# A decoder trunk on one core: gated values of two heads in products of 512 columns, memory tokens normed channel-major, some steps moved

## The chip, the core and the metric

The kernel runs on one core of a Trainium2 chip. The core has a matrix engine (TensorE, in the profile PE, with its weight loads PEld), VectorE (DVE), ScalarE (ACT), GpSimd (POOL) and SyncE (SP), which here only issues transfers. They run side by side, each through its own list of instructions in order, and wait for each other by semaphores. The metric is the device time of one execution in microseconds (us): 835.55 for the kernel before, the median of 3 runs (834.86 to 836.42).

## The reference, cut to what matters

```python
h = rmsnorm(x, g_pre)                       # x: 512 tokens x 1024 channels
gq, gk, gv, ga, gz, dq, dk, dv, iq, ik, iw, dz, xq, xz, gates = split_cols(h @ w_in)
y_gla = gla_mixer(gq, gk, gv, ga, gz, ...)  # 4 heads, chunks of 64; values gv: 256 columns a head
y_dsa = dsa_mixer(dq, dk, dv, iq, ik, iw, dz, rel_bias)  # top-k keys by an indexer
mem_n = rmsnorm(mem, g_mem)                 # 256 memory tokens x 1024 channels
mk, mv = split(mem_n @ w_mem_kv)
y_mem = cross_mixer(xq, xz, mk, mv)
merged = sum(sigmoid(gate) * (y @ w_out) for each branch)
out = x + rmsnorm(merged @ w_o, g_post)
```

All is float32. The norm is y * rsqrt(mean(y * y) + eps) * g over the 1024 channels of a token.

## The kernel before, in words

**Precision.** Each operand of a large product is split in two parts of a faster format: `high` (ScalarE, line 94) rounds, `low` (VectorE, lines 98 and 100) takes the rest. `mm3` (lines 107 to 109) then makes three products: high by high, first operand's high by second's low, low by high. With weights as the second operand its first product needs only whi, its second wlo.

**Weights and units.** Weights come in loads of 1 MB, two buffers (wraw), SyncE's queue. A load has two chunks; `split_next` makes whi (ScalarE) and puts the making of wlo (VectorE) on a list that `flush` works off after the next quarter of TensorE's work has been issued. whi and wlo have four buffers each, so a chunk's split waits until the chunk four before it was used. When a load's second chunk is split, the load after next is issued. Work on TensorE is a list of units of four quarters. A unit of `unit_t` has the channels of a chunk as weights and 512 tokens as moving columns: 24 products of 512 columns. A unit of `unit_n` (gv, dv, mv) has tokens as weights and 256 value columns as moving columns, two tiles of 128 tokens in one PSUM buffer: 48 products of 256 columns for gv, and both chunks of its load are used by each of the load's two units.

**Order.** `at(name, s, fn)` puts a step s quarters behind the start of a unit; s may go past 3, into later units. The loop at the end issues quarter, flush, splits of chunks to come (`need`), then, in the last quarter, the unit's `done`, then the steps of that place:

```python
if s == 1 and u < wo_first:
    need(u + 2)
if s == 3 and u + 2 < wo_first and chunks[u + 2][2]:
    need(u + 3)
```

The order of units at the start is dv, pc (indexer keys, gate inputs), gv0.0, gv0.1, gv1.0, gv1.1, iq0.0, iq0.1, iq1.0, iq1.1, gqk0, gz0, gqk1, gz1, gqk2, gv2, gz2, gqk3, gv3, gz3, dk, dq0. gv0 and gv1 work on x times the gain (gh, gl) and take the norm factor rstd of a token at the end; meanwhile `h_norm` makes the normed hh and hl that all later units use. `gv_done` splits the values to vh and vl. `dv_done` splits the other value products, which stand in four PSUM buffers since the start; `gate_operands` and `gate_log` prepare the forget gate (products pla), `gate_ln` and `gate_sum` finish it.

Of the gated attention's steps `gla_exps`, `gla_q` and `gla_k` (qd, kd, kte, kk) work on a head's gqk, `gla_att` makes its products pa, `gla_turn_k` the transposes tk, `gla_state` the state products kv, `gla_out` the outputs po with their squares, `gla_norm` scales them with GpSimd's rstd, `gla_y` turns and gates them. `score` and `topk_max`, `topk_drop` (16 rounds of three MAX8 and three MATCH_REPLACE8, from gz1.0 on, a step each three quarters) are the indexer's.

**Memory tokens.** `mem_load` (at gate12.0) loads the gain, repeated over the partitions, and two tiles of 128 tokens. At out14 and behind it each tile is squared (`norm_sq`), scaled (`norm_scale`) and turned by eight transposes (`norm_turn`, line 294, xps) into mh and ml, which the units mk and mv use from 559 us on.

**Start.** Channel-major x (xt, four tiles, the first in two halves from ScalarE's queue) and the weights of dv come first, then x token-major (four tiles), whose squares on ScalarE (line 1096) give rstd.

Of the kernel before, what the change touches and what calls it, by code (L numbers as in the profile page):

```python
# [10 lines left out]
F32 = mybir.dt.float32  # L11
# [6 lines left out]
D = 1024  # L18
# [24 lines left out]
for _h in range(4):  # L43
    _pair(f"gqk{_h}", OFF["gq"] + 128 * _h, OFF["gk"] + 128 * _h)
    for _n in ("gv", "gz", "dq", "dz", "xq", "xz"):
        _pair(f"{_n}{_h}", OFF[_n] + 256 * _h, OFF[_n] + 256 * _h + 128)
# [6 lines left out]
NORMAL = ("gv", "dv")  # L53
# [4 lines left out]
def trunk(ctx, tc, x, x_t, mem, w_in, w_c, w_kv, w_out, w_o, cols, g_mem, g_post, w_up, toe, out):  # L58
# [149 lines left out]

    hh = keep.tile([128, KT, T], F32R, name="hh", tag="hh")
# [57 lines left out]
    col = const.tile([128, 14], F32)  # L267
    ba, ggla, gpre = col[:, 0:4], col[:, 4:6], col[:, 6:14]
# [6 lines left out]

    def norm_sq(xt, xn):
        ss = s8("ss", 2)
        for i in range(2):
            act.activation(xn[i], xt[i], AF.Square, scale=1.0 / 32, accum_out=ss[:, i:i + 1])
        return ss  # L280

    def norm_scale(xt, xn, ss, g):
        v = s8("var", 1)
        dve.scalar_tensor_tensor(v, ss[:, 0:1], EPS, ss[:, 1:2], op0=OP.add, op1=OP.add)
        r = rstd_of(v, 1)
        for i in range(2):
            dve.scalar_tensor_tensor(xn[i], xt[i], r[:, 0:1], g[i], op0=OP.mult, op1=OP.mult)

    def norm_turn(xn, dst, tags=("tp", "tp")):
        pts = []  # L290
        for i in range(2):
            p = psum(tags[i], "xps")
            for j in range(4):
                pe.transpose(p[:, 128 * j:128 * j + 128], xn[i][:, 128 * j:128 * j + 128], ident)
            pts.append(p.rearrange("p (k t) -> p k t", k=4))
            high(dst(i)[0], pts[i])
        return lambda: [low(dst(i)[1], pts[i], dst(i)[0]) for i in range(2)]
# [77 lines left out]
    def gv_done(h, i, p):  # L375
        if i == 0:
            GV[h] = [w4(n, F32R).rearrange("p (t d) -> p t d", t=4) for n in ("vh", "vl")]
        vh, vl = GV[h]
        if h < 2:
            for j in range(2):  # L380
                tt = 2 * i + j
                split(vh[:, tt], vl[:, tt], p[:, 256 * j:256 * j + 256], R["rstd"][:, tt:tt + 1])
            return
# [807 lines left out]
```

## Time and profile before

| | before |
|---|---|
| median of 3 runs | 835.55 us |
| the profiled execution | 835.18 us |
| its span, first to last instruction | 833.5 us |
| granted TensorE clock, mean | 0.997 |
| TensorE busy | 818.7 us, 98% |
| weight loads (PEld) | 704.3 us, 85% |
| VectorE busy | 473.8 us, 57% |
| ScalarE busy | 337.1 us, 40% |
| GpSimd busy | 50.2 us, 6% |
| transfers | 86.30 MB, mean 104 GB/s |

Matmuls are pipelined: a product's duration in the profile is longer than the distance from its start to the next one's start, and it is that distance that counts for the stream. VectorE and ScalarE overlap a little too: the next operation starts some 0.1 us ahead of the end of the one before. The clock is TensorE's, as a share of 2.4 GHz; it has two levels, 1.2 and 2.4.

### The profile page before, as it was taken

The numbers are of one execution on the slowest core, as the hardware profiler recorded it, in microseconds if no ns is written. First come the engines' busy times: TensorE is split into PE (matmuls) and PEld (weight loads), VectorE is DVE, ScalarE is ACT, GpSimd is POOL, SyncE is SP. The second block draws the span as 40 slices with busy tenths as digits, with TensorE's granted clock in tenths as the row PEclk, the third lists the DMA queues.
The fourth block names the chain that finished last, engine by engine and source line by source line (L and its number), as shares of the span: only waits on it lengthen the run. The fifth ranks groups of instructions, "written<-read, shape, count | busy, mean of one in ns | idle before, by whom it ended". The sixth has DMA issues, their size and how long they took to land.

```text
span 833.5 us, 10783 instructions
## 1 busy us (share of the span) xinstructions
PE 818.7 (98%) x4320; PEld 704.3 (85%) x4320; DVE 473.8 (57%) x850; ACT 337.1 (40%) x608; POOL 50.2 (6%) x74
## 2 busy tenths in 40 slices
PE   7989999999999999999999999999999999999997
PEld 7989888989888888888888888889989898888885
DVE  4759677888686435446676543545655554343623
ACT  6577554453423223334444422334434343322320
POOL 1000010010000030032131000000000000000000
PEclk9999999999999999999999999999999999999999
DMA  9324121121222231222131125323324142226402
GB/s 332 117 102 138 51 91 62 52 101 53 100 101 101 101 105 73 101 104 99 51 108 71 51 101 176 101 101 101 112 92 147 56 152 70 86 98 223 156 1 102
DMA packets 16387, 86.30 MB, mean 104 GB/s; under 512 B 2064, under 2 KB 2576, under 8 KB 7760
## 3 DMA queue, kind: packets, MB, share of 16 engines
q1 hardware_dynamic: 15328, 84.02, 28.6%
q10 hardware_dynamic: 1008, 1.58, 0.5%
q8 instruction: 34, 0.56, 0.3%
q14 instruction: 17, 0.14, 0.0%
HBM read 82.42 MB, written 2.10 MB: 101 GB/s over the span
## 4 chain that ended last, share of the span: by engine, by line
PE 86%; DVE 5%; ACT 4%; DMA 2%; issue 2%; ACTq 0%; SPq 0%; DVEq 0%; POOLq 0%; POOL 0%
PE out L109 5%; PE out L107 5%; PE out L108 5%; PE pfin L109 2%; PE pfin L108 2%; PE pfin L107 2%; DVE wlo L98 1%; DMA x<-x 1%; PE tpp L721 1%; ACT whi L94 1%; DMA xt<-x_t 1%; PE pov L108 1%; PE pov L109 1%; PE lg L109 1%; PE lg L108 1%
## 5 line engine op out<-in xcount | busy, mean ns | idle before, releaser
L98 DVE TENSOR_TENSOR wlo<-wraw,whi 128x1024 fp32r<-128x1024 f32 (+1 forms) x135 | 163.4, 1211 | 84.4 <-ACT whi L94 83.5
L94 ACT ACTIVATE whi<-wraw 128x1024 fp32r<-128x1024 f32 (+1 forms) x135 | 139.4, 1039 | 22.2 <-PE out L108 19.6
L107 PE MATMUL out<-yh,whi 128*128 128x512 f32 x192 | 75.3, 392 | 0.0
L109 PE MATMUL out<-yh,wlo 128*128 128x512 f32 x192 | 74.8, 390 | 0.0
L108 PE MATMUL out<-yl,whi 128*128 128x512 f32 x192 | 74.8, 389 | 0.0
L707 ACT ACTIVATE bm<-bm,nm 128x128 f32<-128x128 f32 (+3 forms) x32 | 18.0, 564 | 73.6 <-DVE nm L705 71.8
L691 POOL TENSOR_TENSOR bm<-toe,madd 128x128 f32<-128x128 f32 (+3 forms) x32 | 31.0, 986 | 194.6 <-DMA toe<-toe 86.3
L109 PEld LDWEIGHTS out<-yh,wlo 128*128 128x128 f32 x192 | 36.0, 188 | 7.5
L107 PEld LDWEIGHTS out<-yh,whi 128*128 128x128 f32 x192 | 36.1, 188 | 7.3
L108 PEld LDWEIGHTS out<-yl,whi 128*128 128x128 f32 x192 | 36.1, 188 | 7.2
L94 ACT ACTIVATE yh<-th 128x512 fp32r<-128x512 f32 x16 | 10.1, 632 | 44.0 <-DVE th L657 24.9
L512 DVE SCALAR_TENSOR_TENSOR gth<-gth,out 128x512 f32<-128x512 f32 x16 | 11.0, 686 | 28.0 <-PE out L109 28.0
L273 POOL TENSOR_TENSOR rstd<-var,mhalf 128x1 f32<-128x1 f32 x6 | 3.3, 550 | 374.9 <-DVE var L952 289.7
L470 DVE MATCH_REPLACE8 madd<-m,madd 128x256 f32<-128x256 f32 (+2 forms) x48 | 25.6, 543 | 0.0
L466 DVE MAX8 m<-madd 128x8 f32<-128x256 f32 (+2 forms) x48 | 23.6, 546 | 0.0
L705 DVE CUSTOM_DVE_ANT_0 bm<-lg,bm 128x128 f32<-128x128 f32 (+3 forms) x32 | 15.5, 486 | 12.9 <-PE lg L109 12.7
L751 DVE TENSOR_TENSOR ydsa<-pov,th 128x128 f32<-128x128 f32 x32 | 7.8, 286 | 22.5 <-PE pov L109 22.1
L94 ACT ACTIVATE pth<-tpp 128x128 fp32r<-128x128 f32 (+3 forms) x32 | 13.7, 428 | 13.4 <-PE tpp L721 13.4
L456 DVE SCALAR_TENSOR_TENSOR madd<-relu,iw,madd 128x256 f32<-128x256 f32 (+2 forms) x21 | 12.9, 616 | 9.2 <-ACT relu L452 8.9
L949 ACT ACTIVATE sq<-pfin 128x512 f32<-128x512 f32 x8 | 4.8, 598 | 31.5 <-PE pfin L109 31.5
L98 DVE TENSOR_TENSOR yl<-th,yh 128x512 fp32r<-128x512 f32 x16 | 11.1, 693 | 11.2 <-ACT yh L94 11.2
L98 DVE TENSOR_TENSOR ptl<-tpp,pth 128x128 fp32r<-128x128 f32 (+3 forms) x32 | 15.5, 484 | 0.0
(1024 smaller groups left out, 2359.1 us busy)
## 6 DMA issues: line engine op xcount, KB each, us to landing
wraw<-w_in SPq DMA_DIRECT2D x43, 1024.0 KB, 4.8
wraw<-w_out SPq DMA_DIRECT2D x12, 1024.0 KB, 4.8
wraw<-w_kv SPq DMA_DIRECT2D x8, 1024.0 KB, 4.8
wraw<-w_o SPq DMA_DIRECT2D x4, 1024.0 KB, 4.8
x<-x SPq DMA_DIRECT2D x4, 512.0 KB, 8.2
toe<-toe SPq DMA_DIRECT2D x8, 256.0 KB, 5.2
xres<-x SPq DMA_DIRECT2D x4, 512.0 KB, 8.5
xt<-x_t SPq DMA_DIRECT2D x3, 512.0 KB, 7.6
```

The costliest lines, as they stand in the source:

```text
L94: act.activation(hi, src, AF.Copy, scale=scale)
L98: dve.tensor_tensor(lo, src, f(hi), op=OP.subtract)
L107: pe.matmul(o, lh, rh, start=first, stop=False)
L108: pe.matmul(o, lh, rl, start=False, stop=False)
L109: pe.matmul(o, ll, rh, start=False, stop=last)
L456: dve.scalar_tensor_tensor(sc, r[:, :n], iw[:, b, h:h + 1], sc, op0=OP.mult, op1=OP.add)
L466: dve.max(out=M8[b], in_=maskadd[b])
L470: dve.match_replace(out=maskadd[b], in_to_replace=M8[b], in_values=maskadd[b], imm_value=-FMAX)
L512: dve.scalar_tensor_tensor(th, th, 1.0, p, op0=OP.add, op1=OP.mult)
L691: pool.tensor_tensor(bm[:, :n], Q[hp]["toe"][i][:, 384 - 128 * qb:512], maskadd[qb], op=OP.add)
L705: dve.tensor_tensor_reduce(out=bm[:, :n], in0=lg[:, :n], in1=bm[:, :n], scale=-1.0, scalar=FMAX, op0=OP.add, op1=OP.min, accum_out=nm)
L707: act.activation(bm[:, :n], bm[:, :n], AF.Exp, scale=-1.0, bias=nm, accum_out=su)
```

## The change

- **Values of two heads.** gv leaves the pairs of `w_in`; its weights come as `w_gv`, four loads, in chunks of two channel tiles with 512 columns, that is two heads. `wide_units` makes four units for two heads (gvw0.0 to gvw0.3 for heads 0 and 1, gvw1.0 to gvw1.3 for heads 2 and 3), one for each 128 tokens; quarter q of every unit uses the group's chunk q. gvw0 stands where gv0 and gv1 stood; gvw1 stands where gv2 stood, and gv3's place is empty. `gv_done` makes one split of 512 columns per unit; the values lie in tiles of two token tiles by 512 columns, and `gv_of` picks a head's.
- **When chunks are split.** `ahead` replaces the two conditions quoted above: the first chunk of a group at the usual place, the second in the second quarter of the unit before the group, the third in that unit's last quarter, the fourth behind the group's first quarter; none in the next two units; in the group's last unit the next two chunks behind its first and second quarter.
- **Places.** `gate_operands` goes from the third quarter of gv0.1 to the first of gvw0.2, `dv_done` from gv1.0's four quarters to the four from gvw0.2's second on, `gate_log` to gvw0.3's quarters. The third head's `gla_att` and `gla_turn_k` go to gvw1.1; the fourth head gets the places of the second head, in gz3.0 and behind.
- **Memory tokens.** `mem_load` brings two tiles channel-major (`mem_t`) beside two token-major, in place of the repeated gain, which comes with `cols`. The token-major tiles are squared only, one operation of 1024 columns each; GpSimd's power of both; two products with the identity spread the factors over the partitions (`mem_row`, mrps); eight scalings of 256 columns and two splits of 1024 follow, a step a quarter. The transposes go.
- **Start.** The second half of the first xt tile goes to SyncE's queue, behind the first part of dv's weights.

```diff
-    for _n in ("gv", "gz", "dq", "dz", "xq", "xz"):
+    for _n in ("gz", "dq", "dz", "xq", "xz"):
...
-NORMAL = ("gv", "dv")
+NORMAL = ("dv",)
...
+    wide = set()
+
+    def wide_units(name, src, lhs, done):
+
+        first = len(units)
+        wide.add(first)
+        for i in range(2):
+            add_chunks(src[i], None)
+        for tt in range(4):
+            o = []
+
+            def quarter(q, tt=tt, o=o):
+                if q == 0:
+                    o.append(psum("mm", name))
+                wh, wl = chunks[first + q][3]
+                for k in (2 * q, 2 * q + 1):
+                    ah, al = lhs(k, tt)
+                    mm3(o[0], ah, al, wh[:, k % 2], wl[:, k % 2], k == 0, k == KT - 1)
+
+            unit(f"{name}.{tt}", quarter, lambda tt=tt, o=o: done(tt, o[0]))
...
-    col = const.tile([128, 14], F32)
-    ba, ggla, gpre = col[:, 0:4], col[:, 4:6], col[:, 6:14]
+    col = const.tile([128, 22], F32)
+    ba, ggla, gpre, gmem = col[:, 0:4], col[:, 4:6], col[:, 6:14], col[:, 14:22]
...
-    def norm_sq(xt, xn):
-        ss = s8("ss", 2)
-        for i in range(2):
-            act.activation(xn[i], xt[i], AF.Square, scale=1.0 / 32, accum_out=ss[:, i:i + 1])
-        return ss
...
-    def norm_scale(xt, xn, ss, g):
-        v = s8("var", 1)
-        dve.scalar_tensor_tensor(v, ss[:, 0:1], EPS, ss[:, 1:2], op0=OP.add, op1=OP.add)
-        r = rstd_of(v, 1)
-        for i in range(2):
-            dve.scalar_tensor_tensor(xn[i], xt[i], r[:, 0:1], g[i], op0=OP.mult, op1=OP.mult)
-
-    def norm_turn(xn, dst, tags=("tp", "tp")):
-        pts = []
-        for i in range(2):
-            p = psum(tags[i], "xps")
-            for j in range(4):
-                pe.transpose(p[:, 128 * j:128 * j + 128], xn[i][:, 128 * j:128 * j + 128], ident)
-            pts.append(p.rearrange("p (k t) -> p k t", k=4))
-            high(dst(i)[0], pts[i])
-        return lambda: [low(dst(i)[1], pts[i], dst(i)[0]) for i in range(2)]
 
 
...
-    def gv_done(h, i, p):
-        if i == 0:
-            GV[h] = [w4(n, F32R).rearrange("p (t d) -> p t d", t=4) for n in ("vh", "vl")]
-        vh, vl = GV[h]
-        if h < 2:
-            for j in range(2):
-                tt = 2 * i + j
-                split(vh[:, tt], vl[:, tt], p[:, 256 * j:256 * j + 256], R["rstd"][:, tt:tt + 1])
-            return
-        split(vh[:, 2 * i:2 * i + 2], vl[:, 2 * i:2 * i + 2], p.rearrange("p (t d) -> p t d", t=2))
-
-    for h in range(2):
-        win_n(f"gv{h}", lambda i, p, h=h: gv_done(h, i, p), g_lhs)
+    def gv_done(g, tt, p):
+        if tt == 0:
+            GV[g] = [[w4(n, F32R).rearrange("p (t d) -> p t d", t=2) for n in ("vh", "vl")]
+                     for _ in range(2)]
+        vh, vl = GV[g][tt // 2]
+        split(vh[:, tt % 2], vl[:, tt % 2], p, 1.0 if g else R["rstd"][:, tt:tt + 1])
+
+    def gv_of(h, p):
+        return [t[:, p % 2, 256 * (h % 2):256 * (h % 2) + 256] for t in GV[h // 2][p // 2]]
+
+    wide_units("gvw0", [w_gv[0], w_gv[1]], g_lhs, lambda tt, p: gv_done(0, tt, p))
...
-        at("gv1.0", tt, lambda tt=tt: dv_done(tt, R["dvps"][tt]))
+        at("gvw0.2", 1 + tt, lambda tt=tt: dv_done(tt, R["dvps"][tt]))
...
-    at("gv0.1", 2, gate_operands)
+    at("gvw0.2", 0, gate_operands)
     at("iq0.1", 2, turn_iw)
     for h in range(4):
-        at("gv1.1", h, gate_log, h)
+        at("gvw0.3", h, gate_log, h)
...
-        if h > 1:
-            win_n(f"gv{h}", lambda i, p, h=h: gv_done(h, i, p))
+        if h == 2:
+            wide_units("gvw1", [w_gv[2], w_gv[3]], h_lhs, lambda tt, p: gv_done(1, tt, p))
...
     def mem_load():
-        gm = w4("gm")
-        sp.dma_start(gm, bass.AP(tensor=g_mem.tensor, offset=g_mem.offset, ap=[[0, 128], [1, D]]))
-        R["gm"] = gm
-        R["mt"] = []
-        for tt in range(2):
-            mt = w4("mt")
-            sp.dma_start(mt, mem[128 * tt:128 * tt + 128])
-            R["mt"].append(mt)
-        for i in range(2):
+        R["mt"], R["mx"] = [w4("mt") for _ in range(2)], [w4("mx") for _ in range(2)]
+        for i in range(2):
+            sp.dma_start(R["mx"][i], mem[128 * i:128 * i + 128])
+        for i in range(2):
+            sp.dma_start(R["mt"][i], mem_t[:, 1024 * i:1024 * i + 1024])
             mh.append(kv4(f"mh{i}", [4, 256], F32R))
             ml.append(kv4(f"ml{i}", [4, 256], F32R))
-
-    def mem_sq(tt):
-        xt = [R["mt"][tt][:, 512 * i:512 * i + 512] for i in range(2)]
-        xn = [w2("xn") for _ in range(2)]
-        R["mx", tt] = xt, xn, norm_sq(xt, xn)
-
-    def mem_scale(tt):
-        xt, xn, ss = R["mx", tt]
-        norm_scale(xt, xn, ss, [R["gm"][:, 512 * i:512 * i + 512] for i in range(2)])
-
-    def mem_turn(tt):
-        t = slice(128 * tt, 128 * tt + 128)
-        norm_turn(R["mx", tt][1], lambda i: (mh[i][:, :, t], ml[i][:, :, t]))()
+        R["mss"] = s8("mss", 2)
+
+    def mem_sq(i):
+        act.activation(R["mx"][i], R["mx"][i], AF.Square, scale=1.0 / 32,
+                       accum_out=R["mss"][:, i:i + 1])
+
+    def mem_pow():
+        v = s8("mvar", 2)
+        dve.tensor_scalar(v, R["mss"], EPS, None, op0=OP.add)
+        R["mr"] = rstd_of(v, 2)
+
+    def mem_row():
+        p = psum("tp", "mrps")
+        for i in range(2):
+            pe.matmul(p[:, 128 * i:128 * i + 128], R["mr"][:, i:i + 1].to_broadcast([128, 128]),
+                      ident, start=True, stop=True)
+        R["mrow"] = w2("mrow", n=256)
+        act.activation(R["mrow"], p[:, 0:256], AF.Copy)
+
+    def mem_norm(k):
+        t = R["mt"][k // 4].rearrange("p (k t) -> p k t", t=256)
+        dve.scalar_tensor_tensor(t[:, k % 4], t[:, k % 4], gmem[:, k:k + 1], R["mrow"],
+                                 op0=OP.mult, op1=OP.mult)
+        if k % 4 == 3:
+            high(mh[k // 4], t)
+            late.append((low, (ml[k // 4], t, mh[k // 4])))
...
+    def ahead(u, s):
+
+        f = max([w for w in wide if w <= u], default=-9)
+        if u <= f + 2:
+            if (u, s) == (f, 0):
+                need(f + 3)
+        elif u == f + 3:
+            if s < 2:
+                need(f + 4 + s)
+        else:
+            if s == 1:
+                need(u + 2)
+            if s == 3 and (u + 1 in wide or u + 2 < wo_first and chunks[u + 2][2]):
+                need(u + 3)
...
-        if h < 2:
-            at(z + ".0", h, gla_att, h, 0)
-            at(z + ".0", h + 1, gla_att, h, 1)
-            at(z + ".0", h + 2, gla_turn_k, h)
+        if h != 2:
+            d = int(h > 0)
+            at(z + ".0", d, gla_att, h, 0)
+            at(z + ".0", d + 1, gla_att, h, 1)
+            at(z + ".0", d + 2, gla_turn_k, h)
             for p in range(3):
-                at(z + ".1", 2*p + h, gla_state, h, p)
-            after = 6 + h
+                at(z + ".1", 2 * p + d, gla_state, h, p)
+            after = 6 + d
         else:
-            v = f"gv{h}"
-            at(v + ".1", 0, gla_att, h, 0)
-            at(v + ".1", 1, gla_att, h, 1)
-            at(v + ".1", 2, gla_turn_k, h)
+            at("gvw1.1", 0, gla_att, h, 0)
+            at("gvw1.1", 1, gla_att, h, 1)
+            at("gvw1.1", 2, gla_turn_k, h)
             for p in range(3):
                 at(z + ".0", 2+p, gla_state, h, p)
...
-    for tt in range(2):
-        at("out14", 4 * tt, mem_sq, tt)
-        at("out14", 4 * tt + 2, mem_scale, tt)
-        at("out14", 4 * tt + 5, mem_turn, tt)
+    for i in range(2):
+        at("out14", i, mem_sq, i)
+    at("out14", 2, mem_pow)
+    at("out14", 4, mem_row)
+    for k in range(8):
+        at("out14", 6 + k, mem_norm, k)
...
-        for k in range(2):
-            act.dma_start(R["xt"][0][:, k], x_t[:, k])
+        act.dma_start(R["xt"][0][:, 0], x_t[:, 0])
         for k in range(4):
             h, c = k // 2, slice(512 * (k % 2), 512 * (k % 2) + 512)
             sp.dma_start(wdv[:, h, c], loads[0][0][:, h, c])
             if k:
                 sp.dma_start(R["xt"][k], x_t[:, 2 * k:2 * k + 2])
+            else:
+                sp.dma_start(R["xt"][0][:, 1], x_t[:, 1])
...
-                if s == 1 and u < wo_first:
-                    need(u + 2)
-                if s == 3 and u + 2 < wo_first and chunks[u + 2][2]:
-                    need(u + 3)
+                if u < wo_first:
+                    ahead(u, s)
...
+    a["mem_t"] = np.ascontiguousarray(a["mem"].T.reshape(KT, 128, M).transpose(1, 0, 2).reshape(128, KT * M))
...
+    gv = w[:, OFF["gv"]:OFF["gv"] + 1024].reshape(2, 2, 2, 128, 2, 512)
+    a["w_gv"] = np.ascontiguousarray(gv.transpose(4, 0, 3, 1, 2, 5).reshape(4, 128, 2, 1024))
```

## Rows read from the trace of the kernel before

**Rows 1.** The page, part 1: busy time, share of the span, instructions.
```profile
PE 818.7 (98%) x4320; PEld 704.3 (85%) x4320; DVE 473.8 (57%) x850; ACT 337.1 (40%) x608; POOL 50.2 (6%) x74
```
**Rows 2.** Waits of TensorE: us in total, times, longest.
```profile
PE gv1.1_587 L107 <- DVE vl L100: 2.5, 1, 2.5
...
PE gv1.0_521 L108 <- DVE wlo L98: 0.6, 1, 0.6
...
PE pa L580 <- DVE kd L565: 0.2, 1, 0.2
```
**Rows 3.** Windows: stretch, length; PE, PEld, DVE, ACT, POOL busy; clock, DMA, GB/s.
```profile
40.20:57.70 17.50, 14.45 (x103) 13.80 (x102) 11.31 (x18) 12.75 (x24) 0.00 (x0) 0.90 0.18 62
...
123.00:152.20 29.20, 29.20 (x156) 24.59 (x155) 22.03 (x46) 13.44 (x27) 2.14 (x3) 1.00 0.20 71
```
**Rows 4.** Windows, TensorE alone: stretch, length, busy, clock, DMA, GB/s.
```profile
49.50:53.00 3.50, 3.50 (x16) 0.51 0.00 0
```
**Rows 5.** Timeline of TensorE: start, us, what; first products of five units.
```profile
28.66 0.28 PE L107 MATMUL gv0.0_379<-whi,gh 128*128 128x256 f32 x1
...
34.41 0.28 PE L107 MATMUL gv0.1_452<-whi,gh 128*128 128x256 f32 x1
...
491.89 0.39 PE L107 MATMUL gate11.0_4678<-hh,whi 128*128 128x512 f32 x1
...
497.33 0.39 PE L107 MATMUL gate11.1_4709<-hh,whi 128*128 128x512 f32 x1
...
152.21 0.28 PE L107 MATMUL gv2.0_1615<-whi,hh 128*128 128x256 f32 x1
```
**Rows 6.** Timeline of VectorE, 33 to 36 us.
```profile
33.35 1.21 DVE L98 TENSOR_TENSOR wlo<-wraw,whi 128x1024 fp32r<-128x1024 f32 x1
34.49 0.74 DVE L330 SCALAR_TENSOR_TENSOR xt<-xt,col,row 128x512 f32<-128x512 f32 x1
...
35.75 0.74 DVE L330 SCALAR_TENSOR_TENSOR xt<-xt,col,row 128x512 f32<-128x512 f32 x1
```
**Rows 7.** Timeline of ScalarE, 48 to 62 us.
```profile
48.72 1.20 ACT L94 ACTIVATE dvh<-dvps,rstd 128x256 fp32r<-128x256 f32 x3
...
52.80 0.69 ACT L397 ACTIVATE ebig<-pla,col 128x512 f32<-128x512 f32 x1
...
54.46 1.07 ACT L94 ACTIVATE whi<-wraw 128x1024 fp32r<-128x1024 f32 x1
55.41 0.70 ACT L397 ACTIVATE ebig<-pla,col 128x512 f32<-128x512 f32 x1
...
61.83 1.07 ACT L94 ACTIVATE whi<-wraw 128x1024 fp32r<-128x1024 f32 x1
```
**Rows 8.** Timeline of ScalarE, 152 to 153 us.
```profile
152.14 0.84 ACT L647 ACTIVATE on<-po,rstd 128x256 f32<-128x256 f32 x2 [1.13 <-POOL rstd L273]
152.87 0.38 ACT L636 ACTIVATE on<-po 128x256 f32<-128x256 f32 x1
```
**Rows 9.** Timeline of VectorE, 152 to 158 us.
```profile
152.38 1.22 DVE L98 TENSOR_TENSOR wlo<-wraw,whi 128x1024 fp32r<-128x1024 f32 x1
153.51 1.48 DVE L466 MAX8 m<-madd 128x8 f32<-128x256 f32 x3
154.90 0.67 DVE L565 TENSOR_TENSOR kd<-gqk2.1_1549,enb 128x512 f32<-128x512 f32 x1
...
156.65 1.23 DVE L98 TENSOR_TENSOR wlo<-wraw,whi 128x1024 fp32r<-128x1024 f32 x1 [0.22 <-ACT whi L94]
```
**Rows 10.** Timeline of TensorE: transposes of memory tokens, and spreading products rps.
```profile
532.69 1.03 PE L294 MATMUL xps<-ident,xn 128*128 128x128 f32 x8
533.48 0.48 PE L107 MATMUL out<-yh,whi 128*128 128x512 f32 x1
...
23.64 1.05 PE L322 MATMUL rps<-ident,rstd 128*128 128x128 f32 x8
24.45 0.48 PE L107 MATMUL pc<-gh,whi 128*128 128x512 f32 x1
```
**Rows 11.** Timeline of ScalarE: the square of the last tile of x.
```profile
19.19 1.06 ACT L1096 ACTIVATE x<-x 128x1024 f32<-128x1024 f32 x1 [0.59 <-DMA x<-x]
```

More of the change, by code (lines that the diff above doesn't have):

```diff
@@ L52, with trunk @@
         _pair(f"gate{_b}{_j}", _c, _c + 128)
-NORMAL = ("gv", "dv")
+NORMAL = ("dv",)
 PIDX = {n: i for i, (n, _, _) in enumerate(PAIRS)}
 @with_exitstack
-def trunk(ctx, tc, x, x_t, mem, w_in, w_c, w_kv, w_out, w_o, cols, g_mem, g_post, w_up, toe, out):
+def trunk(ctx, tc, x, x_t, mem, mem_t, w_in, w_gv, w_c, w_kv, w_out, w_o, cols, g_post, w_up, toe, out):
     nc = tc.nc
@@ L603, in gla_state @@
         g = G[h]
-        vh, vl = GV[h]
+        vh, vl = gv_of(h, p)
         kv = psum("at", "kv")
         mm3(kv[:, :256], g["kkh"][:, 128 * p:128 * p + 128], g["kkl"][:, 128 * p:128 * p + 128],
-            vh[:, p], vl[:, p])
+            vh, vl)
         S = w2("S", n=256)
@@ L620, in gla_out @@
         g = G[h]
-        vh, vl = GV[h]
         if i == 0:
@@ L629, in gla_out @@
             o = po[:, 256 * j:256 * j + 256]
-            mm3(o, g["ah"][:, p], g["al"][:, p], vh[:, p], vl[:, p], True, p == 0)
+            mm3(o, g["ah"][:, p], g["al"][:, p], *gv_of(h, p), True, p == 0)
             if p:
@@ L1164, in _layout @@
         np.asarray(inputs["g_gla"])[0].reshape(2, 128).T,
-        np.asarray(inputs["g_pre"])[0].reshape(KT, 128).T], axis=1))
-    a["g_mem"] = np.ascontiguousarray(np.asarray(inputs["g_mem"])[0:1])
+        np.asarray(inputs["g_pre"])[0].reshape(KT, 128).T,
+        np.asarray(inputs["g_mem"])[0].reshape(KT, 128).T], axis=1))
     a["g_post"] = np.ascontiguousarray(np.asarray(inputs["g_post"])[0:1])
```

## The prediction

> **What bounds the kernel now.** I read the shares of the engines first: TensorE is busy 98% of the span [rows 1], so the change pays only where TensorE's own stream gets shorter or its few waits go. Next TensorE's waits: 2.5 and 0.6 us ahead of the second head's value units gv1, and 0.2 us at gla_att's products pa [rows 2]. Then the stretches: from 40.2 to 57.7 us TensorE works 14.45 of 17.50 us at a mean granted clock of 0.90, elsewhere it is full; from 123 to 152 VectorE too is busy 22 of 29 us [rows 3]. Last the timelines of VectorE and ScalarE around the gated values, because a TensorE that never waits says nothing of how near the splits of weights (whi on ScalarE, then wlo on VectorE) come to being late. For the mean clock: 3.5 us behind the idle 2.5 us were granted 0.51, the lower of the two levels, 1.2 of 2.4 GHz [rows 4].
>
> A profiled execution took 835.18 us, its span of 833.50 and 1.68 around it; the median of the runs is 835.55, so 0.37 lies between them. The sum is made against 835.18.
>
> **1. Products of 512 columns.** A gv unit of 48 products with 256 columns takes 34.41 - 28.66 = 5.75 us, 119.8 ns each; a unit of 24 with 512 columns takes 497.33 - 491.89 = 5.44 us, 226.7 ns each [rows 5]. 384 of the first (46.0 us) become 192 of the second (43.5 us): -2.5 us of stream, 1.23 in each of the two groups of heads.
>
> The Trainium skill (TensorE: Matmul & The Clock Gate, "Wait — 56ns, not 53.3ns?") gives a matmul its columns at 2.4 GHz and a fixed 2.5 ns. By that, an estimate from the page, joining two products saves 2.6 ns and 192 of them 0.5 us; the rows above have 12.9 ns, and I go by them.
>
> **2. All four weight chunks are due in the first unit of a group.** Before, a unit used two chunks, and the next pair had 11 us more. Now the quarters of gvw0.0 use chunks 3, 4, 5, 6 and those of gvw1.0 four more; units 2 to 4 of a group then need none. A quarter's first product needs only whi; its second needs wlo.
>
> First group. Up to 31.38 all is as before: gvw0.0 starts at 28.66, two quarters take 2.72. Chunk 5's wlo runs at 33.35 and ends at 34.56, then xt and hl take 1.26 (34.49 to 35.75) [rows 6]; chunk 6's wlo, now issued a quarter after gvw0.0's first, follows at 35.75 and ends near 37.0. Its whi is early enough, since ScalarE takes it where it sat idle. So TensorE waits in the third quarter from 31.6 to 34.6 (3.0 us) and in the fourth from 35.9 to 37.0 (1.05), and gvw0.0 ends at 38.15. That is 4.05 us of waiting where there were 3.1 [rows 2] and 1.7 lost to the lower clock (3.5 x 0.49).
>
> From there: gvw0.1 and gvw0.2 bring 49.03. Chunk 7's whi needs the buffer of chunk 3, which gvw0.3's first quarter frees at 50.4, with the drain some 50.6. From here ScalarE is what counts, and I follow its queue: whi 0.95 (54.46 to 55.41), dvh 0.36 (three take 1.20), gate_log 1.66 (52.80 to 54.46), whi 0.95, two gate_log 3.32, vh of 512 columns 0.55 (a third of a gate_log, three such operations), gate_log 1.66 [rows 7], together 9.45: the split of iq1.0's chunk starts at 60.1 where it started at 61.83. ScalarE's and VectorE's work behind it keeps its order through iq, scores and kd, on which pa waits now, so all of it and TensorE come 1.75 us earlier. TensorE alone would be 2.3 earlier (iq0.0 at 55.4 for 57.7); the 0.5 goes into waiting for PSUM buffers of iq and at pa. The later places of gate_operands and dv_done lie where ScalarE now idles, between the splits of gvw0.1 and chunk 7; they cost nothing unless they outlast 50.6. The loads follow the wlo of their buffers: iq1's comes 5 us earlier, gz2's 1.5 us later, with its split 18 us on. Step: -1.75, with its 1.23 of step 1. Bounds: 0 (nothing but a wait given back) to -2.6.
>
> Second group, in the clock of before (all are 1.75 earlier alike). There the second chunk of gv2 was split two quarters earlier than it will be: the order asks for gvw1's second chunk in the second quarter of gqk2.1, the third in its last, the fourth behind gvw1.0's first. ScalarE then has gla_norm's copies ahead of the second chunk, which wait for GpSimd's rstd until 152.14 and end at 152.87 [rows 8]; whi 1.05 brings 153.92, wlo 1.22 brings 155.2. The unit starts at 152.21 [rows 5] and its second quarter needs that at 153.8: 1.4 us of waiting. Behind this wlo VectorE has the top-k maxima (1.39, from 153.51 to 154.90) and gla_k's four operations (1.53, to 156.65 less 0.22 idle) [rows 9], and only then the third chunk's wlo, near 158.0 to 159.2. TensorE's third quarter needs it at 156.6: 2.65 us. The fourth wlo ends at 160.3, when TensorE gets there. So +4.05 against none before, where the wlo at 152.38 landed just in time. Bounds: 0, if VectorE has no backlog (before, no such wait stands in the list), and 5.45, if one more top-k piece of 1.4 gets ahead. With -1.23: **+2.8**.
>
> The third head's attention moves nowhere; the fourth's goes from gv3.1 into gz3.0 and gz3.1, the places of the second head, whose pa waits for nothing now (the one wait of 0.2 is the first head's) [rows 2]. I take 0; bounds 0 to 1.4, one top-k piece in front.
>
> **3. What an idle stretch costs in clock.** The waits of 3.0 and 2.65 us are as long as the one of 2.5 that the lower clock followed [rows 2, 4]; behind the wait of 0.6 it stayed full. If it comes, 3.5 us of stream run at half speed, 1.7 lost. After gvw0.0's first wait a part of that lies in the second, which ends at 37.0 anyway: 0.3 to 1.1. After gvw1.0's nothing hides it: 1.7. I give each an even chance and take +0.9 for both; bounds 0 and 2.8.
>
> **4. Memory tokens.** Two groups of eight transposes take 0.79 each (532.69 to 533.48), and the product behind each 0.09 more [rows 10]. In their place stand two fp32 products of the kind of rps, of which four take 0.81 (23.64 to 24.45) [rows 10]: 0.40. So 1.76 - 0.49 = **-1.3**. Squares, pow, eight scalings of 256 columns and two splits lie beside out14 to gate13.1; the split ends some 14 us ahead of mk0, so the rest costs nothing, and were the cover gone, a late mrow would hold up two products and nothing else before mk0. The transfers are four of 512 KB for three; they go into SyncE's queue some 10 us ahead of the next weights. 0; bounds 0 to 1.3, one such transfer.
>
> **5. Start.** The second half of xt0 goes from ScalarE's queue into SyncE's behind the first weights, 0.4 us of issue there. The first products start about 1 us sooner, but pc waits for ScalarE's squares of x, and the last tile of x, for which ScalarE sat idle 0.59 us before 19.19 [rows 11], still comes behind the same bytes. 0; bounds -0.4 to +0.4, one issue.
>
> **Sum**: -1.75 + 2.8 - 1.3 = -0.25 without the clock, 834.9 us; with 0.9 for it **835.8 us**. The case's own range is 834.2 to 837.2.
>
> **Rivals.**
> Slower: TensorE's clock falls behind both waits, with its full prices 1.1 and 1.7: 834.9 + 2.8 = 837.7, and with a top-k piece more ahead of the third wlo (+1.4) 839.1. For it: the one long wait that the trace has was followed by 0.51. Against: one case is no rule, and in gvw0.0 the two waits may hide all of it. It ends over 837.2 only if gvw1.0's wait carries it too. Chance 0.20.
>
> Faster: VectorE reaches gvw1.0 without backlog, and TensorE waits 1 us there instead of 4.05: 834.9 - 3.05 = 831.9, clock full. For it: VectorE lags because top-k pieces and the states of the second head meet there, and 1.75 us less ahead of them could shift which comes first. Against: that order is written out, and the wait of ScalarE for GpSimd is no backlog. Chance 0.20.
>
> Not what it says: the joined products keep the time of the two, 239.6 ns and not 226.7, because weights come as slices of h in either form; then 2.5 us of saving are missing, 838.3. The Trainium skill's fixed 2.5 ns (same page and section) comes near to that. Against: the rate of a 512-column unit stands in the trace as measured, whatever its weights are. Chance 0.03.
>
> The start carries: x lands earlier than reckoned, and with step 2's upper bound the whole is 835.8 - 0.4 - 0.85 - 0.9 (no lower clock) = 833.6. Chance 0.05.
>
> **How the numbers follow.** The forecast has 0.52. A measurement of this kernel tells about 0.2%, 1.7 us, from no change: 833.9 to 837.2. Faster: 0.20 + 0.05; slower: 0.20 + 0.03; the rest 0.52, that is the forecast's. The range reaches from 832.4, half of the faster rival, to 838.2, into the slower one.
>
> **What would show it.** Right: products of gvw0.0 and gvw1.0 waiting for wlo with 3 to 4 us in each, no wait of TensorE from gvw0.1 to iq0.1, the split of iq1.0's chunk near 60 us, a lower clock right behind one of the waits, unit gvw1.1 without waits at 5.44 plus pa, mrps with four records near 0.4 us. Wrong: gvw1.0 within 6.5 us of its start (the faster rival), pa of the fourth head waiting for kd, a product rate of 512 columns above 0.235 us, or mk0 waiting for ml.

## The result, and the profile after

The changed kernel took 839.58 us, the median of 5 runs (839.28 to 841.70), against 835.34 for the kernel before (5 runs, 834.86 to 836.42): a ratio of 1.0055, 95% interval 1.0043 to 1.0066. That is 4.2 us slower, where I forecast 835.8 and no difference. It lies in what I called the slower rival, and above my range.

The profiled execution is the longest of the five, 841.70 us with a span of 840.0 and a mean clock of 0.992; the other four lie from 839.28 to 840.12 at 0.994. The page's first part, to be set beside [rows 1], says little: TensorE is as full as before.

```profile
PE 820.9 (98%) x4116; PEld 694.9 (83%) x4116; DVE 473.3 (56%) x847; ACT 336.9 (40%) x599; POOL 49.6 (6%) x73
```

TensorE's waits in the changed kernel, as in [rows 2]: what is waited for, us in total, times, longest.

```profile
PE gvw L108 <- DVE wlo L98: 4.7, 4, 2.8
PE pc L107 <- ACT whi L94: 1.6, 1, 1.6
PE kv L109 <- DVE kkl L98: 1.5, 1, 1.5
PE gvw L107 <- ACT whi L94: 1.5, 2, 1.3
```

The 3.1 us of gv1 are gone. In their place products gvw wait 6.2 us for wlo and whi, and two waits are new: pc for its first whi, and the state products kv for kkl.

Windows of TensorE in the changed kernel: stretch, length, busy, granted clock, DMA share, GB/s. The first three are the stretches of 3.4 us at the lower clock; [rows 4] had one. (The last 2 to 4 us of the span are at the lower clock in both kernels, and count in the mean clocks.)

```profile
23.70:27.10 3.40, 3.40 (x13) 0.51 0.84 296
37.40:40.80 3.40, 3.06 (x8) 0.50 0.29 60
160.30:163.70 3.40, 3.39 (x8) 0.50 0.38 128
...
153.27:165.87 12.60, 9.52 (x32) 0.86 0.45 166
165.87:184.21 18.34, 18.34 (x95) 1.00 0.00 1
```

The clock was at 1.2 GHz right behind the wait in pc, behind the long wait in gvw0.0, and inside gvw1.0. The fourth line is gvw1.0 with the first 6 products of the next unit: 30 products, 6.80 us at the 226.7 ns that a 512-column product takes, need 12.60. So 5.80 are lost there, 1.7 to the clock (3.40 x 0.50) and 4.1 to waiting. The last line, the rest of the group, is full.

Timeline of TensorE in the changed kernel, as in [rows 5]: first products behind each wait, and the marks by which I share out the time.

```profile
30.39 0.39 PE L107 MATMUL gvw<-whi,gh 128*128 128x512 f32 x1
...
36.34 0.50 PE L108 MATMUL gvw<-wlo,gh 128*128 128x512 f32 x1 [2.85 <-DVE wlo L98]
...
38.74 0.80 PE L108 MATMUL gvw<-wlo,gh 128*128 128x512 f32 x1 [0.34 <-DVE wlo L98]
...
58.21 0.33 PE L107 MATMUL iq0.0_568<-hh,whi 128*128 128x384 f32 x1
...
153.27 0.39 PE L107 MATMUL gvw<-whi,hh 128*128 128x512 f32 x1
153.50 0.39 PE L108 MATMUL gvw<-wlo,hh 128*128 128x512 f32 x1
...
155.07 0.50 PE L107 MATMUL gvw<-whi,hh 128*128 128x512 f32 x1 [0.28 <-ACT whi L94]
156.33 0.50 PE L108 MATMUL gvw<-wlo,hh 128*128 128x512 f32 x1 [0.76 <-DVE wlo L98]
...
159.02 0.50 PE L107 MATMUL gvw<-whi,hh 128*128 128x512 f32 x1 [1.26 <-ACT whi L94]
160.31 0.79 PE L108 MATMUL gvw<-wlo,hh 128*128 128x512 f32 x1 [0.79 <-DVE wlo L98]
...
223.13 0.39 PE L109 MATMUL kv<-vh,kkl 128*128 128x256 f32 x1 [1.54 <-DVE kkl L98]
...
257.57 0.39 PE L107 MATMUL dz0.1_2355<-hh,whi 128*128 128x512 f32 x1
...
521.46 0.39 PE L107 MATMUL gate12.0_4606<-hh,whi 128*128 128x512 f32 x1
...
539.14 0.61 PE L802 MATMUL mrps<-ident,rstd 128*128 128x128 f32 x4
539.50 0.48 PE L107 MATMUL out<-yh,whi 128*128 128x512 f32 x1
...
565.46 0.28 PE L107 MATMUL mk0.0_4898<-mh,whi 128*128 128x256 f32 x1
```

The same marks in the trace of before, with its first pa:

```profile
57.69 0.34 PE L107 MATMUL iq0.0_672<-hh,whi 128*128 128x384 f32 x1
...
89.34 0.68 PE L580 MATMUL pa<-qd,kd 128*128 128x128 f32 x4 [0.16 <-DVE kd L565]
...
249.93 0.39 PE L107 MATMUL dz0.1_2555<-hh,whi 128*128 128x512 f32 x1
...
513.65 0.39 PE L107 MATMUL gate12.0_4806<-hh,whi 128*128 128x512 f32 x1
...
558.95 0.28 PE L107 MATMUL mk0.0_5122<-mh,whi 128*128 128x256 f32 x1
```

By difference, in this execution, the changed kernel is 1.06 behind at gvw1.0 (153.27 for 152.21, [rows 5]), 7.64 behind at dz0.1 (257.57 for 249.93), and 6.51 behind at mk0 (565.46 for 558.95). So the second group of heads cost 6.6 us, and between gate12.0 and mk0 the memory part gained 1.3 (44.00 us for 45.30). The 1.06 has the stretch of lower clock in pc in it, which, to judge by their mean clocks, the other four executions don't have.

Timeline of ScalarE in the changed kernel around gvw1.0, as in [rows 8].

```profile
153.23 0.84 ACT L642 ACTIVATE on<-po,rstd 128x256 f32<-128x256 f32 x2 [1.13 <-POOL rstd L294]
153.96 1.06 ACT L94 ACTIVATE whi<-wraw 128x1024 fp32r<-128x1024 f32 x1
...
157.18 0.84 ACT L642 ACTIVATE on<-po,rstd 128x256 f32<-128x256 f32 x2 [1.43 <-POOL rstd L294]
157.91 2.00 ACT L94 ACTIVATE whi<-wraw 128x1024 fp32r<-128x1024 f32 x2
```

Timeline of VectorE in the changed kernel, there and ahead of kv, as in [rows 9].

```profile
155.05 1.23 DVE L98 TENSOR_TENSOR wlo<-wraw,whi 128x1024 fp32r<-128x1024 f32 x1 [1.50 <-ACT whi L94]
...
159.03 2.36 DVE L98 TENSOR_TENSOR wlo<-wraw,whi 128x1024 fp32r<-128x1024 f32 x2
...
216.45 0.75 DVE L652 SCALAR_TENSOR_TENSOR th<-to,col,th 128x512 f32<-128x512 f32 x1
...
218.50 0.73 DVE L583 COPY_PREDICATED attz<-cmask,pa 128x512 f32<-128x512 uint8 x1
219.94 0.69 DVE L98 TENSOR_TENSOR al<-attz,ah 128x512 fp32r<-128x512 f32 x1 [0.70 <-ACT ah L94]
220.55 1.47 DVE L462 MAX8 m<-madd 128x8 f32<-128x256 f32 x3
221.94 0.67 DVE L486 SCALAR_TENSOR_TENSOR th<-th,gz3.0_1950 128x512 f32<-128x512 f32 x1
222.53 0.55 DVE L98 TENSOR_TENSOR kkl<-tk,kkh 128x384 fp32r<-128x384 f32 x1
```

At gvw1.0 each of two whi stands on ScalarE behind gla_norm's copies, which wait 1.13 and 1.43 us for GpSimd. At gz3.1 the fourth head's kkl stands on VectorE behind the end of the third head's output (th, yl), the mask, al, three MAX8 and a gate: it ends at 223.08, and TensorE has stood for it since 221.6.

### The profile page after: what moved, and what is told of

It is laid out like the page before. It is cut to its first block, busy times and chain, and to the rows that moved or that the text cites. A ratio compares the mean times of both kernels' runs of the same rounds, so it can differ in the third digit from the quotient of the medians.

```text
span 840.0 us, 10350 instructions
## 1 busy us (share of the span) xinstructions
PE 820.9 (98%) x4116; PEld 694.9 (83%) x4116; DVE 473.3 (56%) x847; ACT 336.9 (40%) x599; POOL 49.6 (6%) x73
## 4 chain that ended last, share of the span: by engine, by line
PE 83%; DVE 8%; ACT 4%; issue 2%; DMA 2%; SPq 0%; POOL 0%; DVEq 0%; POOLq 0%; ACTq 0%
PE out L107 5%; PE out L109 5%; PE out L108 5%; DVE wlo L98 2%; PE pfin L109 2%; PE pfin L108 2%; PE gvw L108 2%; PE pfin L107 2%; PE gvw L109 1%; PE gvw L107 1%; DMA x<-x 1%; ACT whi L94 1%; PE tpp L716 1%; DMA wraw<-w_in 1%; DVE m L462 1%
## 5 line engine op out<-in xcount | busy, mean ns | idle before, releaser
L108 PE MATMUL gvw<-wlo,gh 128*128 128x512 f32 x32 | 13.2, 414 | 3.2 <-DVE wlo L98 3.2
```

Of the source, the lines that this page charges most:

```text
L108: pe.matmul(o, lh, rl, start=False, stop=False)
```

## The experiments

Theory A after the result: the loss is the second group, where four chunks are due in one unit (waits, the lower clock behind them) and where the fourth head's new places make kv wait. Theory B: the new start, whose wait in pc brings the lower clock, carries the loss. The first four runs do one part of the change alone, on the kernel before.

**Memory alone.** The change's memory part, nothing else.

```diff
-            p = psum(tags[i], "xps")
-            for j in range(4):
-                pe.transpose(p[:, 128 * j:128 * j + 128], xn[i][:, 128 * j:128 * j + 128], ident)
...
+        p = psum("tp", "mrps")
+        for i in range(2):
+            pe.matmul(p[:, 128 * i:128 * i + 128], R["mr"][:, i:i + 1].to_broadcast([128, 128]),
+                      ident, start=True, stop=True)
```

> The kernel before with the memory tokens' part alone (channel-major load, no transposes). Theory A (the loss is made by weight chunks that are due too early in gvw1, and by the fourth head's new place) and theory B (the loss is made at the start, by the moved load of x and the idle time it leaves ahead of pc) expect the same: 1.3 us less than before, 834.0, with mrps near 0.4 us where the transposes took 1.6 in all.

834.25 us (11 runs) beside 835.38 for before, ratio 0.9987 (0.9978 to 0.9996): 1.1 us less.

**Start alone.**

```diff
-        for k in range(2):
-            act.dma_start(R["xt"][0][:, k], x_t[:, k])
+        act.dma_start(R["xt"][0][:, 0], x_t[:, 0])
...
+            else:
+                sp.dma_start(R["xt"][0][:, 1], x_t[:, 1])
```

> The kernel before with the second half of the first xt tile in SyncE's queue alone. Theory A: no change, 835.3 within 0.4, and idle time ahead of pc but no lower clock there in most executions. Theory B: 1.6 us more, 836.9, because the products of dv end earlier, TensorE idles ahead of pc and its clock falls there, as in the profile of the changed kernel.

835.58 us (11 runs), ratio 1.0005 (0.9996 to 1.0014): nothing in the median. Eight executions took 835.02 to 835.81; three took 836.46 to 836.92, which is theory B's time, so the start may cost some executions about 1.5 us. It doesn't make the 4.2, and theory B falls.

**First group alone.** gvw0 in place of gv0 and gv1, with `ahead` and the moved gate_operands, dv_done and gate_log.

```diff
-    for h in range(2):
-        win_n(f"gv{h}", lambda i, p, h=h: gv_done(h, i, p), g_lhs)
+    wide_units("gvw0", [w_gv[0], w_gv[1]], g_lhs, lambda tt, p: gv_done(0, tt, p))
```

> The kernel before with gvw0 alone (heads 0 and 1 in products of 512 columns, splits of chunks as in the change; heads 2 and 3 as before). Theory A: gvw0.0 waits some 4 us for wlo, a lower clock behind it costs about 1.1, and the whole is 0.6 to 1.7 us faster than before, 833.6 to 834.7. Theory B: what is lost is lost ahead of gvw0, so this is 1.7 us faster, 833.6.

834.82 us (11 runs), ratio 0.9991 (0.9982 to 0.9999): 0.6 less. The median hides two cases: the four executions at a mean clock of 0.996 took 833.65 to 834.09, 1.3 to 1.7 less than before, the seven at 0.992 to 0.995 took 834.64 to 836.21. The profiled one, of the first four, had no lower clock in gvw0.0. TensorE's waits in gvw0.0, timeline of this kernel:

```profile
34.57 0.50 PE L110 MATMUL gvw<-wlo,gh 128*128 128x512 f32 x1 [2.85 <-DVE wlo L100]
36.97 0.50 PE L110 MATMUL gvw<-wlo,gh 128*128 128x512 f32 x1 [0.74 <-DVE wlo L100]
```

**Second group alone.** gvw1 in place of gv2 and gv3, `ahead`, and the fourth head's places.

```diff
-        if h > 1:
-            win_n(f"gv{h}", lambda i, p, h=h: gv_done(h, i, p))
+        if h == 2:
+            wide_units("gvw1", [w_gv[2], w_gv[3]], h_lhs, lambda tt, p: gv_done(1, tt, p))
...
-        if h < 2:
+        if h != 2:
```

> The kernel before with gvw1 alone, and with the fourth head's steps at their new places (heads 0 and 1 as before). Theory A: gvw1.0 waits 4 us for wlo and a lower clock follows (1.7), kv of the fourth head waits 1.5 to 1.8 for kkl, products save 1.2: 6.3 us slower, 841.6. Theory B: at most 3 us slower, 838.3.

842.58 us (4 runs, 841.69 to 843.99), ratio 1.0087 (1.0073 to 1.0101): 7.2 more, the whole loss of the change and over. A window of its trace (us, then PE, PEld, DVE, ACT and POOL busy, clock, DMA, GB/s):

```profile
158.53:165.36 6.83, 6.32 (x14) 4.65 (x15) 3.97 (x9) 1.34 (x2) 0.00 (x0) 0.50 0.64 234
```

Its waits of TensorE:

```profile
PE kv L111 <- DVE kkl L100: 1.5, 1, 1.5
PE gvw L109 <- ACT whi L96: 1.5, 2, 1.3
...
PE gvw L110 <- DVE wlo L100: 1.3, 2, 0.8
```

Nearly the same waits, and here the lower clock lasted twice as long, 6.83 us. The first 30 products took 13.57 us (152.82 to 166.39) for 12.60 in the change, so the longer stretch cost 1.0. The four parts sum to -1.1 + 0.2 - 0.6 + 7.2 = 5.7; the change measured 4.2. The longer stretch may be part of that difference, but this profile is the longest of its four executions; where the 1.5 us lie is not shown.

The next four change the changed kernel.

**The fourth head's states later**, by two quarters.

```diff
-                at(z + ".1", 2 * p + d, gla_state, h, p)
-            after = 6 + d
+                at(z + ".1", 2 * p + d + (2 if h == 3 else 0), gla_state, h, p)
+            after = 6 + d + (2 if h == 3 else 0)
```

> The changed kernel with the fourth head's state products and outputs two quarters later. Theory: kv's wait of 1.5 us for kkl, which lies behind a top-k maximum and the gating of the third head on VectorE, goes, and nothing takes its place: 1.8 us less than the changed kernel, 837.8. Rival: VectorE is late by its whole queue there and the wait comes back at the next state or output: 839.6.

839.22 us (5 runs, 837.51 to 839.62), ratio 1.0038 (1.0026 to 1.0051); kv's wait is gone. The medians don't tell 839.22 from 839.58. But the executions differ in how often the clock fell, and like must be set beside like. Its profiled execution has the same three stretches of lower clock as that of the change and a span of 837.5 where that had 840.0. Of these 2.5 us 0.7 are there at gz3.0 already (208.99 for 209.67); from gz3.0 to dq0.0 it takes 28.80 for 30.62, the 1.8 that kv lost. By mean clock: at 0.993 it took 839.22 to 839.62, where the change at 0.992 took 841.70; at 0.995 it took 837.51 and 837.99, where the change at 0.994 took 839.28 to 840.12. So the theory holds, as far as these few executions tell, and the medians hid it.

**Splits earlier**: gvw1's second chunk in the last quarter of gqk2.0, its third in the second of gqk2.1.

```diff
+        if u > 2 and (u + 2 in wide and s == 3 or u + 1 in wide and s == 1):
+            need(u + 3)
+            return
```

> The changed kernel with gvw1's second chunk split a unit before (last quarter of gqk2.0) and its third in the second quarter of gqk2.1, the fourth as it is. Theory (the order of splits makes the wait): the second and third wlo come in time, the fourth, now behind the maximum and gla_k, is late by 2.7 us; wait 2.7 for 4.1, so 1.3 less, 838.3, and 836.6 if the lower clock goes with it. Rival (VectorE's backlog makes the wait, whatever the order): 839.6.

838.58 us (5 runs, 836.21 to 838.94), ratio 1.0036 (1.0022 to 1.0050). In gvw1.0 TensorE waited for the last chunk alone, 1.25 us for its whi and 0.79 for its wlo, 2.5 with the products' restarts; the theory had 2.7. In the execution profiled, 836.21 at a mean clock of 0.997, the clock stayed up there; the other four took 838.19 to 838.94 at 0.994 and 0.995, so there it probably fell. These are near the theory's two times, 836.6 and 838.3.

**Waits filled.** In the first unit of a group 11 products (gvw0.0) and 5 and 10 (gvw1.0) of 512 columns, whose result nothing uses, stand where TensorE waited (FILL is 1 in this run).

```diff
+FILLS = {"gvw0": (0, 0, 11, 0), "gvw1": (0, 5, 10, 0)}
...
+                n = FILLS[name][q] if FILL and tt == 0 else 0
+                if n:
+                    x = psum("tp", "fill")
+                    for i in range(n):
+                        pe.matmul(x, gh[0][:, 0:128] if name == "gvw0" else hh[:, 0, 0:128],
+                                  gh[0] if name == "gvw0" else hh[:, 0], start=True, stop=True)
```

> The changed kernel with products into an unused PSUM buffer put where gvw0.0 and gvw1.0 wait (11 ahead of gvw0.0's third quarter, 5 and 10 ahead of gvw1.0's second and third, 0.227 us each, within the waits). Theory (the lower clock behind each wait costs 1.1 and 1.7 us): clock full through both, same waits less the filling, 836.8. Rival (the lower clock is hidden, since VectorE and ScalarE decide): 839.6 or more.

837.40 us (10 runs, 837.05 to 839.52), ratio 1.0027 (1.0018 to 1.0036): 2.2 less than the change, with useless work added. The span and mean clock of its profile:

```profile
core 0: 835.7 us, clock 0.999
```

Its waits of TensorE for weights of the groups:

```profile
PE gvw L112 <- DVE wlo L102: 1.3, 3, 0.7
```

The weights come no earlier, so what went is the clock's part: behind waits of 0.7 us and less in both groups it stayed at 2.4 GHz. By the marks the gain lies where the clock had fallen: gvw0.0 to iq0.0 takes 26.86 us for 27.82 in the change, gvw1.0 to gz2.0 29.36 for 30.94.

**Pairs.** Two token tiles run through the four chunks together, so a chunk is due every half unit; gvw1's splits come earlier, gate_operands one unit, the fourth head's states two quarters later.

```diff
+                def quarter(q, a=a, half=half, o=o):
+                    j, c = q % 2, 2 * half + q // 2
+                    if c == 0:
+                        o[j] = psum(PTAG[name][2 * a + j], name)
+                    wh, wl = chunks[first + c][3]
+                    for k in (2 * c, 2 * c + 1):
+                        ah, al = lhs(k, 2 * a + j)
+                        mm3(o[j], ah, al, wh[:, k % 2], wl[:, k % 2], k == 0, k == KT - 1)
```

> The changed kernel with the four units of a group taken as two pairs of token tiles, each chunk used for both tiles of a pair ahead of the next chunk (a second PSUM buffer per pair), gvw1's second and third chunk split a unit earlier as in splits_earlier, gate_operands earlier, and the fourth head's states two quarters later. Theory (chunks due every 1.36 us are what made the waits; at 2.7 us the splits keep up): no wait over 0.6 us in gvw0 and gvw1, no lower clock behind them, the split of iq1.0's chunk near 56 us instead of 61.8, products save 1.2 in the second group, memory tokens 1.3: 828 to 830. Rival (ScalarE and VectorE have no time for it before 89 us whatever TensorE's order): 833 to 834.

834.61 us (11 runs), ratio 0.9988 (0.9979 to 0.9996): 5.0 less than the change, but not the time expected. gvw1 had no wait at all. In gvw0 the second pair's last tile got the PSUM buffer of the first tile and waited for its split. The first of TensorE's waits:

```profile
PE gvw L111 <- DVE vl L104: 4.1, 1, 4.1
```

The window of TensorE behind it (us, busy, clock, DMA, GB/s):

```profile
47.10:50.50 3.40, 3.40 (x8) 0.51 0.00 0
```

The timeline of VectorE at its end:

```profile
46.26 1.40 DVE L104 SCALAR_TENSOR_TENSOR vl<-gvw,rstd,vh 128x512 fp32r<-128x512 f32 x2
```

The splits vl ran at 46.26, behind the normed x, and the lower clock followed.

The last four build on this.

**Pairs with other buffers.** The second pair takes the two buffers `tp`, which nothing else uses there.

```diff
-PTAG = {"gvw0": ("mm", "mm", "tp", "mm"), "gvw1": ("mm", "ac", "mm", "mm")}
+PTAG = {"gvw0": ("mm", "mm", "tp", "tp"), "gvw1": ("mm", "ac", "mm", "mm")}
```

> The kernel of pairs with one edit: in the first group the last two of the four token tiles take the two tp buffers of PSUM, so no product has to wait for the split of the first two tiles. Theory A (what is left of the loss in pairs is that one wait of 4.1 us, with the lower clock behind it, 1.7 us): 834.6 - 5.8 = 828.8 us, range 828.3 to 830.5, no wait over 1 us of a gvw product, no lower clock behind one. Rival (behind it the split of iq0's first chunk or the normed x is late, so the wait only moves to iq0.0): 832 to 834.6, with a wait of iq0 for wlo or hl of 2 us or more.

828.08 us (4 runs, 827.79 to 829.48), ratio 0.9917 (0.9903 to 0.9930): 7.3 us faster than before, 11.5 faster than the change. Its longest wait of TensorE behind the first unit:

```profile
PE pc L111 <- ACT whi L98: 1.0, 1, 1.0
```

Windows of TensorE in it: the first group, and gvw1's first 30 products.

```profile
28.48:52.13 23.65, 23.31 (x102) 1.00 0.28 100
146.63:153.43 6.80, 6.80 (x31) 1.00 0.46 154
```

Group one takes 23.65 us to iq0.0 where before took 29.03 (28.66 to 57.69); gvw1's first 30 products take the bare 6.80, at the full clock. No wait of gvw is left. By the marks the first group gives 5.4 us against before, the stretch from gvw1.0 to dz0.1 0.7 (97.05 for 97.72), the memory part 1.3 (44.00 for 45.30). That the buffers matter is shown by this run beside the one above; what the earlier gate_operands is worth in it was not tried alone.

**The same with the start of before.** Both halves of the first xt tile from ScalarE's queue again.

```diff
-        act.dma_start(R["xt"][0][:, 0], x_t[:, 0])
+        for k in range(2):
+            act.dma_start(R["xt"][0][:, k], x_t[:, k])
...
-            else:
-                sp.dma_start(R["xt"][0][:, 1], x_t[:, 1])
```

> The kernel of pairs_buffers with the start of the kernel before (both halves of the first xt tile from ScalarE's queue). Theory A (the start carries nothing either way): the time of pairs_buffers within 0.4 us, 828.4 to 829.2 if that gives 828.8. Rival (the start of the change makes TensorE idle 1.6 us before pc and so costs a lower clock in pc in part of the executions): 0.8 to 1.7 us less than pairs_buffers.

828.23 us (4 runs, 827.85 to 828.47), ratio 0.9915 (0.9901 to 0.9928): 0.15 from the run above, no difference. In the median the start is worth nothing either way.

**Second group in pairs alone**, with the memory part and the fourth head's later states; the first group and the start as before (`gn_done` is before's `gv_done`).

```diff
-    wide_units("gvw0", [w_gv[0], w_gv[1]], g_lhs, lambda tt, p: gv_done(0, tt, p))
+    for h in range(2):
+        win_n(f"gv{h}", lambda i, p, h=h: gn_done(h, i, p), g_lhs)
```

> The kernel before with the memory tokens of the change and the second group alone in products of 512 columns, its chunks due one at a time for two token tiles (half a unit apart), the fourth head's states and outputs two quarters later than in the change; first group, its places and the start as before. Theory A (products 1.2 us less in the group, memory 1.1 us less, nothing lost): 835.4 - 2.3 = 833.1 us, range 832.6 to 833.7, no wait of gvw for wlo. Rival (the 1.2 us of the products are given back at the fourth head or at pa): 834.2 or more.

833.89 us (11 runs, 833.41 to 835.31), ratio 0.9986 (0.9977 to 0.9995): 1.5 less, 0.8 short of the theory, between both. Its trace has no wait of gvw. From gvw1.0 to dz0.1 it takes 97.05 us for 97.72 before, so half of the products' 1.2 comes back, in no wait. Summing the distances from each product's start to the next shows where: gv's products take 22.49 us for 23.70, but those of gz, dz and dk and the transposes `to` take 0.76 more, those of dq 0.24 less. The fourth head's steps now stand between products of gz3 and behind, where they stood between those of gv3; that this is the reason was not tested.

**The change's first group, the second in pairs**: the kernel above, with gvw0 as in the change.

```diff
-    for h in range(2):
-        win_n(f"gv{h}", lambda i, p, h=h: gn_done(h, i, p), g_lhs)
+    wide_units("gvw0", [w_gv[0], w_gv[1]], g_lhs, lambda tt, p: gv_done(0, tt, p))
```

> As second_group_pairs, but the first group as in the changed kernel (all four chunks due in its first unit). Theory A (the first group alone was worth -0.6): 833.1 - 0.6 = 832.5 us, range 831.8 to 833.3, waits of gvw for wlo 3.5 to 4 us in the first group and none in the second. Rival (with the memory and the later kernel in phase with it, the lower clock behind the first group's waits costs its 1.7 us in most executions): 833.5 to 834.5.

833.34 us (8 runs, 831.76 to 834.79), ratio 0.9975 (0.9965 to 0.9985): 0.55 less than the run above, as first_group_alone gave, though the two intervals overlap; just over theory A's range and short of the rival's. Both have a part in it: two executions at a mean clock of 0.997 took 831.76 (the profiled one, with no lower clock in gvw0.0) and 831.87, the other six, at 0.992 to 0.995, took 832.77 to 834.79. So without the lower clock the first group gains about what was forecast, and in most executions, to judge by their mean clocks, the lower clock takes a part back. The median is 6.2 less than the change, from the order of the second group, the fourth head's later states and the old start, which costs nothing.

## Why the prediction was wrong

**What bounds the kernel, and products of 512 columns (step 1): right.** The distance of two products in gvw0.0 and gvw1.0 is 226.7 ns (153.27 to 153.50 and on). The rival that they keep the time of two falls. The Trainium skill's fixed 2.5 ns (TensorE: Matmul & The Clock Gate, "Wait — 56ns, not 53.3ns?") makes 215.8 ns of 512 columns, an estimate from the page, and does not hold for these streams, with 226.7 and a weight load for each product. By it joining two would save 2.5 ns, again an estimate, not the 2.6 that I wrote. In the second group, though, only 0.67 of the 1.23 us is left at dz0.1 even where no product of the group waits (second_group_pairs).

**The first group (step 2): right in mechanism and size.** I had waits of 3.0 and 1.05; the traces have 2.85 and 0.34 to 0.75 idle. I had -1.75 without the clock: in change_then_pairs, whose profile has no lower clock there, the first pa comes 59.07 us behind gvw0.0's start, in before 60.68, so -1.6. These are its marks:

```profile
28.68 0.39 PE L111 MATMUL gvw<-whi,gh 128*128 128x512 f32 x1
...
55.53 0.33 PE L111 MATMUL iq0.0_568<-hh,whi 128*128 128x384 f32 x1
...
87.75 0.68 PE L655 MATMUL pa<-qd,kd 128*128 128x128 f32 x4
```

The split of iq1.0's chunk, which I had near 60 us, started at 60.16 in first_group_alone. With the clock, gvw0.0 to iq0.0 takes 27.82 in the change for 26.85 there: 1.0 us, the upper end of my 0.3 to 1.1 (0.7 in the profile of states_later, 0.5 in that of splits_earlier), and the median of the group alone moved by -0.6.

**The second group's waits (step 2): right to 0.1.** Forecast 4.05, measured 4.1 (3.1 idle, the rest the products' restarts), by the queue I named: copies that wait for GpSimd, then whi, wlo, MAX8 and gla_k. Only the pieces differ. I had the third quarter wait for wlo alone; in the trace it waits 1.26 for whi and 0.79 more for wlo, since ScalarE's whi stood behind a second pair of copies (157.18).

**The fourth head's move (step 2): the first step that failed.** I took 0, bounds 0 to 1.4, with pa as what might wait. What waited was kv, 1.8 us with the products' restart (221.19 to 223.35 for three products that took 0.35). I had followed the third head's values but not its output. With gv3's place empty, the third head's second output step (th, yl) stands one quarter ahead of the step that makes the fourth head's kkl, where it stood four quarters ahead, and the first state products come two quarters behind that step instead of four. So VectorE had more to do in front of kkl than the one top-k piece I allowed for, and less time for it. The states two quarters later wait for nothing.

**The clock (step 3): the second step that failed.** I gave each wait an even chance and took 0.9 of a possible 2.8. In the change both fell, at 37.40 and 160.30, about 1.0 and 1.7. For gvw0.0 the even chance was no bad guess: behind the same 2.85 us the clock fell in the profiled executions of the change, of states_later and of splits_earlier, not in those of first_group_alone and change_then_pairs. For gvw1.0 it was a bad one: in the three profiles where all its waits stood together (the change, states_later, second_group_alone) the clock fell every time, once for twice the time, though no idle stretch there is over 1.26; in that of splits_earlier, with the last two waits alone, it stayed up.

**Memory (step 4): right.** -1.3 in the trace, -1.1 alone; mrps take 0.36 where I had 0.40. **Start (step 5): right**: 0.2 us in start_alone and 0.15 in pairs_old_start, both within the interval. It went as I had it: dv's products wait less at the start, and then pc waits 1.6 us for its first whi, which ScalarE makes behind the squares of x. Only the first product came 0.14 us sooner (7.18 for 7.32), not 1. What I had not seen is that the lower clock can follow pc's wait, as in the change's profiled execution; in start_alone's, with 1.5 us of the same wait, it did not.

So of the 3.8 us between forecast and median, kv accounts for 1.8 and the clock for 1.8 (1.0 + 1.7 for 0.9); 0.2 is left. The slower rival at 839.1 had the place and the price of the clock, but drew its last 1.4 us from a top-k piece ahead of the third wlo, where no such thing happened; the time agrees by luck, by the wrong term. Its 0.20 was too little: my own list had 4.05 us of waiting within gvw1.0, and I priced the clock by the longest wait alone.

## What to carry to other kernels

Joining two streams of products makes twice as many weights due in one unit: in gvw1.0 the lateness and the clock behind it cost 5.8 us, more than twice what all the wider products save by their rate (2.5). Let two outputs run through each chunk in turn, give them PSUM buffers that nothing slow must empty first, and, with the splits, gate_operands and the fourth head's states moved to suit, the same change gains 7.3 us. When a unit is taken out of the order, list every step on each engine's queue that moves closer to another, not only those that the change names.

## What was not expected of the hardware

The clock fell behind waits that differ (2.85 us at once; 0.28, 0.76, 1.26 and 0.79 in 6 us; 1.6 in pc) and stayed up behind the same 2.85 in two other profiles. Behind pc's wait with the new start it fell in three of seven profiles, after 1.6, 1.2 and 1.5 us, and not after 1.5, 1.4, 1.3 and 1.0; with the old start it fell among dv's products, 9 to 12 us into the span, in six of seven. So the length of the last wait alone doesn't decide. 15 useless products in gvw1.0's waits and 11 in gvw0.0's kept 2.4 GHz and made the kernel 2.2 us faster. What decides between the two outcomes is not settled by these runs.
